# Hybrid decoder trunk on one core: score pieces of their own width, and a last tile whose second half runs in two pieces

## The chip, the cores and the metric

The kernel runs on one core of a Trainium2 chip. The core has five engines that each follow a stream of instructions of their own: PE (TensorE, matrix products; the loading of its weights is listed apart, as PEld), DVE (VectorE), ACT (ScalarE), POOL (GpSimd) and SP (SyncE, which here only issues DMAs). They meet through semaphores. The metric is the device time of one execution in microseconds (us), and the median of several executions is what counts.

## The reference

One layer of a decoder trunk over 1024 tokens of width 1024: differential softmax attention with 8 heads beside gated linear attention with 4 heads, both on one set of input projections, then one output projection, a normalisation, and the residual.

```python
h = rms_norm(x, pre_g)
z = h @ w_in                                  # all projections at once
# per attention head, for two maps (m = 0, 1), causal:
p_m = softmax(where(mask, q_m @ k_m.T, -inf))
oa  = (p_0 - lam * p_1) @ v                   # then rms_norm and a gate
ob  = gla_chunked(...)                        # then rms_norm and a gate
y = concatenate([oa, ob]) @ w_out             # 1024 x 2048 @ 2048 x 1024
return x + rms_norm(y, post_g)
```

## The kernel before

**Precision.** All large products are made from operands split into a high and a low part in the type fp32r, with three matmuls a product (high x high, low x high, high x low). Each matmul has 128 x 128 weights and streams up to 512 columns into one of the eight PSUM banks; a bank holds 128 x 512 fp32.

**Stages.** From 0 to 620 us the kernel normalises x and makes the input projections (by a Strassen-like scheme of seven products). From 620 to 925 us it runs attention. From 925 to 971 us it finishes the eight output tiles of 128 rows, and the rest is the end of the last of them.

**Attention** (620 to 925 us). Three generators are run against each other by `merge` (called at L1517 with their costs): `all_scores`, `all_values` and `out_early`. `scores(h, qb)` treats one block of 128 queries of one head: it needs `n = (qb + 1) * 128` keys, and `parts_of(n)` (L1114) says in which pieces of columns the scores are made. A piece is one PSUM bank `sc`. Each half of it takes two matmuls, `q` and `qs` against `k`. DVE then adds the mask and takes the minimum (L1168), ACT takes the exponential (L1178), DVE takes reciprocals (L1203), POOL scales the second map (L1204), and DVE subtracts it from the first (L1208). `parts_of` rounds a piece up to at least 256 columns: for `qb` 0 (n = 128) the matmuls are 256 columns wide, and for `qb` 4 (n = 640) the second piece is (512, 768). The readers of the bank take `e = min(b, n)`, so they never read the surplus columns. `values(h, j)` transposes the finished weights on PE (`wtr`, L114), and multiplies them with v into `po`; `out_early` makes the parts of the output projection that need no attention result (`ypart`).

The costs that `merge` weighs are `c = 0.08 + (e - a) / 512 * 0.56` per piece, worked out from `e`, not from the padded width. The instructions that `mm` issues stay in the order in which they are written; those of the other engines are placed by a scheduler, unless `pin` or `issue_after` ties them.

**End tiles.** `ENDS = [4, 5, 6, 7, 0, 1, 2, 3]` is the order in which tiles of rows are finished. `seed` copies what `out_early` had put aside for a tile into one of the eight PSUM banks in turn (`banks`), and `last_times` adds the last products: for one half `dh` (512 columns of the output, one bank) and one block `e` of the mixed heads, three matmuls of 512 columns. `finish(n)` (L1558) does this for e = 4 to 7 and both halves, 24 matmuls, called `yps` in the profile. After each half ACT squares the bank and sums the squares along the row (L1567, with a second small instruction that reads the sum). `rstd` (L1600) then makes the reciprocal root: Ln and Exp on ACT (L1602, L1603), and on DVE a half of the sum (L1604) and two steps of refinement (L1606, L1612). The minus one that the last refinement leaves is in `post_g`.

For the last two tiles the product with `post_g` does not wait for the root: DVE multiplies the bank by `post_g` into `y` (L1573 for the first half, L1577 for the second, tied behind the `half` of L1604), and then one operation per half scales y by the root and adds x (L1586). SP stores each half with a DMA of 256 KB (L1589).

Of the kernel before, what the change touches and what calls it, by code (L numbers as in the profile page):

```python
# [8 lines left out]
F32 = mybir.dt.float32  # L9
F32R = mybir.dt.float32r  # L10
AF = mybir.ActivationFunctionType
ALU = mybir.AluOpType
PSUM = bass.MemoryType.PSUM

P = 128
S = 1024
D = 1024
NT = S // P
# [4 lines left out]
EPS = 1e-6  # L23
# [8 lines left out]
def hymba_kernel(  # L32
# [20 lines left out]
    nc = tc.nc  # L53
    act, dve, pool, pe, sp = nc.scalar, nc.vector, nc.gpsimd, nc.tensor, nc.sync
# [4 lines left out]
    def cols(half):  # L59
        return slice(half * 512, half * 512 + 512)  # L60


    const = ctx.enter_context(tc.tile_pool(name="const", bufs=1))
# [46 lines left out]
    def mm(*a, **k):  # L110
        tc.keep_in_program_order(pe.matmul(*a, **k))  # L111
# [86 lines left out]
    y, z = len(pairs) - 2, len(pairs) - 1  # L198
# [910 lines left out]
    def pin(first, ins):  # L1109

        if first:
            tc.keep_in_program_order(ins)

    def parts_of(n):  # L1114
        return [(0, max(n, 256))] if n <= 512 else [(0, 512), (512, max(n, 768))]

    def load_v(h):
        v = [smp.tile([P, NT, P], F32R, tag="v", name=f"v{t}", bufs=4) for t in range(2)]
# [19 lines left out]
    w, used, scored, opened = {}, set(), [], {}  # L1138

    def scores(h, qb):  # L1140
# [5 lines left out]
        p1 = smp.tile([P, S], F32, tag="p1", name="p1", bufs=2)  # L1146
        for m, p in enumerate((p0, p1)):
            parts = parts_of(n)
            if h == DA_HEADS - 1 and (qb, m) in ((1, 1), (0, 0), (0, 1)):

# [237 lines left out]
    def out_early():  # L1388
# [63 lines left out]
        for st in ENDS[:2]:  # L1452
            for dh in range(2):
                for e in range(4, 7):
                    last_times(st, dh, parts_d[st], e)
                    yield 0.69
            if st == ENDS[0]:
                mix_pair(2)
                for dh in range(2):
                    yp = smp.tile([P, 512], F32, tag="yst", name="yp", bufs=2)  # L1460
                    sp.dma_start(yp, yd[ENDS[2]][dh])
                    yp2.append(yp)
                seed(ENDS[2], 0, SC[2], yp2[0])
# [10 lines left out]
    def early_ends():  # L1474

        for e in range(4, 7):
            last_times(ENDS[2], 0, parts_d[ENDS[2]], e)
        for n, st in enumerate(ENDS[:2]):
            last_part(ENDS[n + 1], parts_d[ENDS[n + 1]])
            if not n:  # L1480
                seed(ENDS[2], 1, PO, yp2[1])
            for dh in range(2):
                last_times(st, dh, parts_d[st], 7)


    parts_d, ps_d, yp2 = {}, {}, []
# [12 lines left out]
        opened[b] = None  # L1499
        pin(b not in Y, act.copy(ps, yp))  # L1500

    def last_times(st, dh, part, e):
        mh, ml = part
        hi, lo = wo[e]
        for i, (a, b) in enumerate(((mh, hi), (ml, hi), (mh, lo))):
            mm(
                ps_d[st, dh], a[:, e - 4, :], b[:, cols(dh)],
                start=False, stop=(e == 7 and i == 2), skip_group_check=True,
            )

    T = 8 * 36.0
    LAG = 21.0
    s_cost = sum(
        2 * sum(0.08 + (min(b, n) - a) / 512 * 0.56 for a, b in parts_of(n)) + 0.25 + n / 1024 * 1.4
        for n in range(P, S + 1, P)
    )
# [8 lines left out]
    fin = ctx.enter_context(tc.tile_pool(name="fin", bufs=3, reuse_waits="tile"))  # L1525
    post_g = fin.tile([P, D], F32, name="post_g", bufs=1)
# [4 lines left out]
    raws_d, yps, xts = {}, {}, {}  # L1531
# [26 lines left out]
    def finish(n):  # L1558
        st = ENDS[n]
        rows = slice(st * P, (st + 1) * P)  # L1560
        y = fin.tile([P, D], F32, name="y")
        ssq = const.tile([P, 4, 1], F32, tag="end_ssq", name="ssq", bufs=3)
        for dh in range(2):
            for e in range((8, 8, 7 - 3 * dh)[n] if n < 3 else 4, 8):
                last_times(st, dh, parts_d[st], e)
            junk = fin.tile([P, 512], F32, name="junk", bufs=2)
            pin(True, act.activation(  # L1567
                junk, ps_d[st, dh], AF.Square, scale=D**-0.5, accum_out=ssq[:, 2 + dh]
            ))
            if not dh:  # L1570
                dve.tensor_scalar(ssq[:, 0], ssq[:, 2], EPS, None, ALU.add)
                if n >= NT - LAST:
                    dve.tensor_tensor(y[:, cols(0)], ps_d[st, 0], post_g[:, cols(0)], ALU.mult)  # L1573
        ins = rstd(nc, ssq, ssq[:, 3], ssq[:, 0])[2]
        if n >= NT - LAST:
            with tc.issue_after(ins.ins):
                dve.tensor_tensor(y[:, cols(1)], ps_d[st, 1], post_g[:, cols(1)], ALU.mult)  # L1577
        for dh in range(2):
            cs = cols(dh)
            if n < NT - LAST:  # L1580
                dve.scalar_tensor_tensor(
                    y[:, cs], ps_d[st, dh], ssq[:, 1], post_g[:, cs], ALU.mult, ALU.mult
                )
                pool.dma_start(out[0, rows, cs], y[:, cs], accum_op=ALU.add)
            else:
                dve.scalar_tensor_tensor(  # L1586
                    y[:, cs], y[:, cs], ssq[:, 1], xts[n][:, cs], ALU.mult, ALU.add
                )
                sp.dma_start(out[0, rows, cs], y[:, cs])  # L1589

    for n in range(4):
        fetch(n)
    for n in range(NT):
        prime(n + 2)
        fetch(n + 4)
        finish(n)


def rstd(nc, t, s, eps, pin=None):

    pin = pin or (lambda ins: ins)
    pin(nc.scalar.activation(t[:, 1], s, AF.Ln, bias=eps))  # L1602
    exp = pin(nc.scalar.activation(t[:, 1], t[:, 1], AF.Exp, scale=-0.5))  # L1603
    half = pin(nc.vector.tensor_scalar(t[:, 2], s, eps, 0.5, ALU.add, ALU.mult))  # L1604
    if t.shape[2] == 1:
        pin(nc.vector.scalar_tensor_tensor(  # L1606
            t[:, 2], t[:, 1], t[:, 2], t[:, 1], ALU.mult, ALU.mult
        ))
    else:
        pin(nc.vector.tensor_tensor(t[:, 2], t[:, 2], t[:, 1], ALU.mult))  # L1610
        pin(nc.vector.tensor_tensor(t[:, 2], t[:, 2], t[:, 1], ALU.mult))
    last = nc.vector.scalar_tensor_tensor(  # L1612
        t[:, 1], t[:, 2], 1.5, t[:, 1], ALU.subtract, ALU.mult
    )
    return exp, pin(last), half
# [32 lines left out]
```

## Time and profile before

| | us |
|---|---|
| three executions | 978.89, 980.10, 977.54 |
| median | 978.89 |
| the profiled execution: its own time | 979.4 |
| the profiled execution: its span | 977.7 |

The span runs from the first to the last record, so 1.7 us of the profiled execution lie around it. The page's other views follow in the prediction, beside the sentences that use them. In a row of the timeline stand the start, the duration, the engine, the line, the operation, output <- inputs, and the tile's shape; a bracket at its end gives the idle time before it and who ended that. In a row of the page's groups stand the count, the busy time in us, the mean of one in ns, and the idle time before them. In a row of the windows stand the stretch and its length, then the busy time and count of PE, PEld, DVE, ACT and POOL, the granted clock of TensorE, the busy share of the DMA engines, and the GB/s that they moved.

### The profile page before, as it was taken

The page shows a single profiled execution, that of the slowest core. Times are in us where ns is not written, and L with a number is a line of the kernel's source. Part 1 is how long each engine was busy: PE and PEld are TensorE (multiplying, and loading weights), DVE is VectorE, ACT ScalarE, POOL GpSimd, SP SyncE. Part 2 cuts the span into 40 slices and gives each one's busy share as a digit, 9 for nine tenths or more (in the row PEclk, how much of TensorE's full clock was granted, in tenths as well). Part 3 has the DMA queues.
Part 4 walks back from the last instruction along what each step waited for, and adds up shares of the span by engine and source line. Part 5 has one row for each costly group of instructions (what it writes and reads, how often), then busy time and mean ns, then how long its engine had stood idle before and what let it go on. Part 6 is the DMA issues. An engine that isn't in the chain of part 4 may idle for free.

```text
span 977.7 us, 14802 instructions
## 1 busy us (share of the span) xinstructions
PE 956.5 (98%) x4866; PEld 807.0 (83%) x4866; DVE 738.5 (76%) x1450; ACT 590.2 (60%) x1152; POOL 210.2 (21%) x289
## 2 busy tenths in 40 slices
PE   6999999999999999999989999999999999999997
PEld 4888888878888888888878888888888888888875
DVE  5996576889989776778787766677787778887755
ACT  7741232347466467756577774367667667787764
POOL 5420100011211121112110000022232233443232
PEclk9999999999999999999999999999999999999999
DMA  8255543758865775899986569998575678994658
GB/s 305 83 161 160 194 143 99 223 167 268 278 234 191 265 249 195 268 279 301 310 258 194 172 216 320 396 329 253 165 245 181 199 265 245 327 267 99 198 156 156
DMA packets 144556, 220.37 MB, mean 225 GB/s; under 512 B 14704, under 2 KB 78704, under 8 KB 144384
## 3 DMA queue, kind: packets, MB, share of 16 engines
q1 hardware_dynamic: 130144, 175.38, 56.3%
q0 software_dynamic: 14336, 44.05, 15.2%
q8 instruction: 38, 0.62, 0.3%
q14 instruction: 38, 0.31, 0.1%
HBM read 133.93 MB, written 88.60 MB: 228 GB/s over the span
## 4 chain that ended last, share of the span: by engine, by line
PE 91%; ACT 3%; DVE 3%; DMA 2%; issue 1%; DVEq 0%; POOL 0%; ACTq 0%; SPq 0%
PE x L111 16%; PE v L111 16%; PE ypart L111 12%; PE z L111 11%; PE y L111 11%; PE sc L111 7%; PE po L111 5%; PE yps L111 4%; PE wtr L114 3%; PE gpo L111 2%; PE kv L111 1%; PE gkl_ps L111 1%; PE ms L111 1%; DMA m_raw<-mixd 1%; PE pa L111 1%
## 5 line engine op out<-in xcount | busy, mean ns | idle before, releaser
L1178 ACT ACTIVATE p<-p,stt 128x896 f32<-128x896 f32 (+7 forms) x128 | 99.3, 777 | 47.1 <-DVE stt L1168 44.2
L335 DVE TENSOR_TENSOR w<-w_raw,w 128x512 fp32r<-128x512 f32 x134 | 91.8, 688 | 31.5 <-ACT w L333 31.0
L333 ACT CAST w<-w_raw 128x512 fp32r<-128x512 f32 x134 | 82.5, 619 | 42.7 <-PE y L111 19.4
L1204 POOL TENSOR_SCALAR p<-p,stt,lam 128x1024 f32<-128x1024 f32 (+3 forms) x64 | 54.9, 858 | 207.9 <-DVE stt L1203 202.1
L1168 DVE CUSTOM_DVE_ANT_0 p<-sc,maskt 128x512 f32<-128x512 f32 (+3 forms) x128 | 74.4, 584 | 31.6 <-PE sc L111 30.9
L111 PE MATMUL y<-h_hi,w 128*128 128x512 f32 x320 | 80.6, 394 | 0.0
L111 PE MATMUL x<-s_hi,w 128*128 128x512 f32 x320 | 80.5, 394 | 0.0
L111 PE MATMUL z<-s_hi,w 128*128 128x512 f32 x320 | 80.4, 393 | 0.0
L111 PE MATMUL ypart<-wo_hi,m_hi 128*128 128x512 f32 x192 | 79.4, 413 | 0.6 <-ACT yst L1385 0.5
L111 PE MATMUL v<-w,s_hi 128*128 128x512 f32 x256 | 79.0, 390 | 0.1
L111 PE MATMUL ypart<-wo_hi,m_lo 128*128 128x512 f32 x192 | 75.5, 393 | 0.0
L111 PE MATMUL ypart<-wo_lo,m_hi 128*128 128x512 f32 x192 | 75.5, 393 | 0.0
L488 ACT COPY s<-x 128x512 f32<-128x512 f32 x60 | 35.0, 583 | 63.1 <-PE x L111 62.9
L111 PE MATMUL sc<-k,q 128*128 128x512 f32 (+1 forms) x192 | 71.0, 372 | 0.4 <-DVE stt L1168 0.4
L111 PEld LDWEIGHTS z<-s_hi,w 128*128 128x128 f32 x320 | 59.1, 188 | 11.7
L111 PEld LDWEIGHTS x<-s_hi,w 128*128 128x128 f32 x320 | 59.1, 188 | 11.7
L111 PEld LDWEIGHTS y<-h_hi,w 128*128 128x128 f32 x320 | 59.0, 188 | 11.6
L111 PE MATMUL sc<-k,qs 128*128 128x512 f32 (+1 forms) x192 | 66.6, 349 | 0.0
L285 ACT CAST w<-w_block 128x1024 fp32r<-128x1024 f32 x24 | 25.0, 1051 | 66.0 <-PE v L111 43.1
L257 DVE TENSOR_TENSOR w_raw<-w_raw 128x512 f32<-128x512 f32 x80 | 55.2, 690 | 9.9 <-DMA w_raw<-in_w_in_dram 8.9
L111 PE MATMUL v<-w,h_hi 128*128 128x512 f32 x192 | 60.3, 401 | 0.4 <-ACT h_hi L582 0.4
L1208 DVE SCALAR_TENSOR_TENSOR p<-p,stt,p 128x1024 f32<-128x1024 f32 (+3 forms) x64 | 52.5, 824 | 6.7 <-POOL p L1204 6.5
(233 smaller groups left out, 2379.5 us busy)
## 6 DMA issues: line engine op xcount, KB each, us to landing
w_raw<-in_w_in_dram SPq DMA_DIRECT2D x40, 512.0 KB, 5.2
w_block<-in_w_in_dram SPq DMA_DIRECT2D x16, 512.0 KB, 4.4
wo_raw<-in_w_out_dram POOLq DMA_DIRECT2D x32, 256.0 KB, 4.2
wo_d<-wo_hi POOLq DMA_DIRECT2D x32, 256.0 KB, 4.4
wo_d<-wo_raw POOLq DMA_DIRECT2D x32, 256.0 KB, 4.8
qs<-q_d SPq DMA_DIRECT2D x32, 256.0 KB, 8.1
k<-k_d SPq DMA_DIRECT2D x16, 512.0 KB, 9.1
q<-q_d SPq DMA_DIRECT2D x16, 512.0 KB, 6.8
```

Of the source, the lines that this page charges most:

```text
L111: tc.keep_in_program_order(pe.matmul(*a, **k))
L114: tc.keep_in_program_order(pe.transpose(dst, src, ident))
L257: dve.tensor_tensor(dst, a, b, ALU.subtract)
L285: act.copy(w[0], src)
L333: act.copy(w[0], src)
L335: split_last[:] = [dve.tensor_tensor(w[1], src, fp(w[0]), ALU.subtract)]
L488: act.copy(b[k], ps)
L1168: ins = dve.tensor_tensor_reduce(p[:, a:e], sc[:, : e - a], maskt[:, NZ + P - (e - a) :] if last else maskt[:, : e - a], 1.0, 3e38 if i == ...
L1178: act.activation(p[:, :n], p[:, :n], AF.Exp, bias=st[:, m : m + 1], scale=-1.0, accum_out=st[:, 2 + m : 3 + m],)
L1204: pool.tensor_scalar(p1[:, :n], p1[:, :n], st[:, 5:6], lam, ALU.mult, ALU.mult)
L1208: dve.scalar_tensor_tensor(p0[:, :n], p0[:, :n], st[:, 4:5], p1[:, :n], ALU.mult, ALU.subtract)
```

## The change

It has two parts.

**Part 1.** `parts_of` returns the pieces without padding. A piece of 128 columns is then made with matmuls of 128 columns. Head 7 keeps its written exceptions of 512 columns for `(qb, m)` = (1, 1), (0, 0) and (0, 1).

**Part 2.** The last tile (n = 7) no longer goes through `finish` but through `finish_last`. Its second half is made in two pieces of 256 columns, each with twelve matmuls of 256 columns. Each piece has its own square and its own product with `post_g`. After the root is there, the final scaling is divided: ACT scales columns 0 to 191 into a tile `z`, POOL adds x to it, and DVE treats columns 192 to 639 and 640 to 1023 as before. SP stores 640 columns (320 KB) and then 384 (192 KB).

```diff
     def parts_of(n):
-        return [(0, max(n, 256))] if n <= 512 else [(0, 512), (512, max(n, 768))]
+        return [(0, n)] if n <= 512 else [(0, 512), (512, n)]
...
-    def last_times(st, dh, part, e):
+    def last_times(st, dh, part, e, a=0, b=512):
         mh, ml = part
         hi, lo = wo[e]
-        for i, (a, b) in enumerate(((mh, hi), (ml, hi), (mh, lo))):
+        at = slice(512 * dh + a, 512 * dh + b)
+        for i, (m, w) in enumerate(((mh, hi), (ml, hi), (mh, lo))):
             mm(
-                ps_d[st, dh], a[:, e - 4, :], b[:, cols(dh)],
+                ps_d[st, dh][:, a:b], m[:, e - 4, :], w[:, at],
                 start=False, stop=(e == 7 and i == 2), skip_group_check=True,
             )
...
         ssq = const.tile([P, 4, 1], F32, tag="end_ssq", name="ssq", bufs=3)
+        if n == NT - 1:
+            return finish_last(st, rows, y, ssq, xts[n])
...
+    def finish_last(st, rows, y, ssq, xt):
+        junk = [fin.tile([P, 512], F32, name="junk", bufs=2) for _ in range(2)]
+        part = const.tile([P, 3], F32, name="last_ssq")
+        r, ys = ssq[:, 1], [(0, 0, 512), (1, 0, 256), (1, 256, 512)]
+        for i, (dh, a, b) in enumerate(ys):
+            for e in range(4, 8):
+                last_times(st, dh, parts_d[st], e, a, b)
+            ps = ps_d[st, dh][:, a:b]
+            pin(True, act.activation(
+                junk[dh][:, a:b], ps, AF.Square, scale=D**-0.5, accum_out=part[:, i : i + 1]
+            ))
+            if i == 1:
+                dve.scalar_tensor_tensor(
+                    ssq[:, 0], part[:, 0:1], EPS, part[:, 1:2], ALU.add, ALU.add
+                )
+            if i < 2:
+                at = slice(512 * dh + a, 512 * dh + b)
+                last = dve.tensor_tensor(y[:, at], ps, post_g[:, at], ALU.mult)
+        ins = rstd(nc, ssq, part[:, 2:3], ssq[:, 0])[2]
+        with tc.issue_after(ins.ins):
+            dve.tensor_tensor(y[:, 768:], ps, post_g[:, 768:], ALU.mult)
+        z = fin.tile([P, 192], F32, name="z", bufs=1)
+        act.activation(z, y[:, :192], AF.Copy, scale=r)
+        pool.tensor_tensor(y[:, :192], z, xt[:, :192], ALU.add)
+        for a, b in ((192, 640), (640, 1024)):
+            dve.scalar_tensor_tensor(y[:, a:b], y[:, a:b], r, xt[:, a:b], ALU.mult, ALU.add)
+        sp.dma_start(out[0, rows, :640], y[:, :640])
+        sp.dma_start(out[0, rows, 640:], y[:, 640:])
```

In the changed program the Square stands on L1602, the sum of parts on L1606, the products with `post_g` on L1611 (the first two pieces) and L1614 (the third), the new ACT and POOL steps on L1616 and L1617, the last scaling on L1619 and the stores on L1620 and L1621; `rstd` is at L1634 (Ln), L1635 (Exp), L1636, L1638 and L1644.

What the two parts move is seen in the order of the built programs. First PE in the attention stage, a piece of the difference between the two programs. `sc` is the bank of a scores piece, `k_5898` and `q_5894` are buffers of one head's keys and queries, and `wtr` is a transposition for `values`.

```order
 L111 MATMUL sc<-k_5896,q_5894 128x512
 L111 MATMUL sc<-k_5896,qs_5900 128x512
-L111 MATMUL sc<-k_5898,q_5894 128x256
-L111 MATMUL sc<-k_5898,qs_5900 128x256
+L111 MATMUL sc<-k_5898,q_5894 128x128
+L111 MATMUL sc<-k_5898,qs_5900 128x128
 L114 MATMUL wtr<-ident,p_6292 128x128
 L114 MATMUL wtr<-ident,p_6197 128x128
```

Nothing moved: the pair of `qb` 4 stands where it stood, and each of its matmuls is 128 columns narrower. The same holds of all 60 matmuls that the padding had widened (28 of `qb` 0 in heads 0 to 6, and 32 of `qb` 4 in heads 0 to 7). Behind them five neighbouring pairs of rows on DVE and two on ACT have changed places.

Second PE at the end of the program, around the start of the last tile's second half. The bracket names the counters that an instruction waits for; DVE_49 counts what DVE has finished. Before:

```order
L111 MATMUL yps<-wo_hi,m_lo 128x512 [waits DVE_49]
L111 MATMUL yps<-wo_lo,m_hi 128x512
L111 MATMUL yps<-wo_hi,m_hi 128x512 [waits Activation_49]
L111 MATMUL yps<-wo_hi,m_lo 128x512
L111 MATMUL yps<-wo_lo,m_hi 128x512
```

Of the change, around the start of the third piece, twelve matmuls after the row that waits for Activation_49:

```order
L111 MATMUL yps<-wo_hi,m_hi 128x256
L111 MATMUL yps<-wo_hi,m_lo 128x256
L111 MATMUL yps<-wo_lo,m_hi 128x256
L111 MATMUL yps<-wo_hi,m_hi 128x256 [waits DVE_49]
L111 MATMUL yps<-wo_hi,m_lo 128x256
L111 MATMUL yps<-wo_lo,m_hi 128x256
```

The row with the wait is the third piece's first matmul. It is new: the value of the counter that it waits for is reached when the second piece's product with `post_g` (L1611) is finished, since both pieces lie in one PSUM bank.

Third DVE, from the end of the last tile's first half to the end of the program. Before:

```order
L1571 TENSOR_SCALAR ssq<-ssq 128x1 [waits Activation_49]
L1573 TENSOR_TENSOR y<-yps,post_g 128x512 [waits DMASW7_49,DMASW6_49]
L1604 TENSOR_SCALAR ssq<-ssq 128x1 [waits DVE_49,Activation_49]
L1577 TENSOR_TENSOR y<-yps,post_g 128x512
L1606 SCALAR_TENSOR_TENSOR ssq<-ssq 128x1 [waits DVE_49,Activation_49]
L1612 SCALAR_TENSOR_TENSOR ssq<-ssq 128x1 [waits DVE_49]
L1586 SCALAR_TENSOR_TENSOR y<-y,ssq,xt 128x512 [waits DMAHW4_49,DVE_49]
L1586 SCALAR_TENSOR_TENSOR y<-y,ssq,xt 128x512
```

Of the change:

```order
L1611 TENSOR_TENSOR y<-yps,post_g 128x512 [waits DMASW7_49,DMASW6_49,Activation_49]
L1606 SCALAR_TENSOR_TENSOR ssq<-last_ssq 128x1 [waits Activation_49]
L1611 TENSOR_TENSOR y<-yps,post_g 128x256
L1636 TENSOR_SCALAR ssq<-last_ssq,ssq 128x1 [waits Activation_49]
L1614 TENSOR_TENSOR y<-yps,post_g 128x256
L1638 SCALAR_TENSOR_TENSOR ssq<-ssq 128x1 [waits DVE_49,Activation_49]
L1644 SCALAR_TENSOR_TENSOR ssq<-ssq 128x1 [waits DVE_49]
L1619 SCALAR_TENSOR_TENSOR y<-y,ssq,xt 128x448 [waits DMAHW4_49,DVE_49]
L1619 SCALAR_TENSOR_TENSOR y<-y,ssq,xt 128x384
```

The second piece's product with `post_g` stands behind the sum of parts, which waits for ACT's square of that piece; the product that stood behind the last half now covers 256 columns; and the two scalings cover 832 columns of the 1024. The other 192 go through ACT and POOL. SP's first store of the last tile waits for both DVE and POOL, its second for DVE alone.

## The prediction

> **What bounds the kernel now.** The first view is the busy time of the engines, the second the chain that ended last.
>
> ```profile
> PE 956.5 (98%) x4866; PEld 807.0 (83%) x4866; DVE 738.5 (76%) x1450; ACT 590.2 (60%) x1152; POOL 210.2 (21%) x289
> PE 91%; ACT 3%; DVE 3%; DMA 2%; issue 1%; DVEq 0%; POOL 0%; ACTq 0%; SPq 0%
> ```
>
> PE is busy for 98% of the span and holds 91% of the chain: an edit counts by what it takes from or adds to PE's stream, and by what it does after PE's last matmul. The two parts lie in two stages, so the third view is the windows of these two.
>
> ```profile
> 620.00:925.00 305.00, 303.34 (x1748) 262.60 (x1747) 230.47 (x632) 210.39 (x468) 100.37 (x118) 1.00 0.77 241
> 971.20:977.70 6.50, 0.00 (x0) 0.00 (x0) 2.51 (x6) 1.19 (x4) 0.00 (x0) 0.77 0.21 81
> ```
>
> In attention PE idles for 305.00 - 303.34 = 1.66 us in all, at a granted clock of 1.00: fewer PE cycles there shorten the kernel directly. In the last 6.5 us PE does nothing, and a chain through ACT, DVE and SP sets the end; the timeline shows it.
>
> ```profile
> 968.31 0.39 PE L111 MATMUL yps<-wo_hi,m_hi 128*128 128x512 f32 x1
> ...
> 970.81 0.39 PE L111 MATMUL yps<-wo_lo,m_hi 128*128 128x512 f32 x1
> 971.23 0.60 ACT L1567 ACTIVATE junk<-yps 128x512 f32<-128x512 f32 x1 [2.03 <-PE yps L111]
> 971.73 0.19 ACT L1567 ACTIVATION_READ_ACCUMULATOR junk<-yps 128x1 f32 x1
> 971.95 0.30 ACT L1602 ACTIVATE ssq<-ssq 128x1 f32<-128x1 f32 x1
> 971.95 0.21 DVE L1604 TENSOR_SCALAR ssq<-ssq 128x1 f32<-128x1 f32 x1 [1.95 <-ACT junk L1567]
> 972.08 0.68 DVE L1577 TENSOR_TENSOR y<-yps,post_g 128x512 f32<-128x512 f32 x1
> 972.28 0.20 ACT L1603 ACTIVATE ssq<-ssq 128x1 f32<-128x1 f32 x1
> 972.68 0.21 DVE L1606 SCALAR_TENSOR_TENSOR ssq<-ssq 128x1 f32<-128x1 f32 x1
> 972.93 0.16 DVE L1612 SCALAR_TENSOR_TENSOR ssq<-ssq 128x1 f32<-128x1 f32 x1
> 973.12 1.41 DVE L1586 SCALAR_TENSOR_TENSOR y<-y,ssq,xt 128x512 f32<-128x512 f32 x2
> 973.90 0.99 SPq L1589 DMA_DIRECT2D out_dram<-y  x2
> ```
>
> The first two rows are the first and the last of the second half's twelve matmuls. The square takes 971.23 to 971.92, the root 971.95 to 973.09, the two scalings 0.705 us each, and the stores are issued at 973.90 and at the second scaling's end, 973.12 + 1.41 = 974.53.
>
> **Part 1: narrower scores.** 60 matmuls go from 256 to 128 columns. What does one save?
>
> ```profile
> 748.02 0.28 PE L111 MATMUL sc<-k,q 128*128 128x256 f32 x1
> 748.14 0.28 PE L111 MATMUL sc<-k,qs 128*128 128x256 f32 x1
> 748.26 0.40 PE L111 MATMUL ypart<-wo_hi,m_hi 128*128 128x512 f32 x1
> 651.78 0.22 PE L111 MATMUL po<-wt_lo,v 128*128 128x128 f32 x1
> 651.84 0.45 PE L111 MATMUL ypart<-wo_hi,m_hi 128*128 128x512 f32 x1
> 652.12 0.40 PE L111 MATMUL ypart<-wo_hi,m_lo 128*128 128x512 f32 x1
> L111 PE MATMUL po<-wt_hi,v 128*128 128x128 f32 x64 | 10.7, 249 | 0.0
> ```
>
> Starts are what counts, since matmuls overlap. A matmul of 256 columns takes a slot of (748.26 - 748.02) / 2 = 0.12. The one of 128 columns at 651.78 lets the next start after 0.06, but that one, of 512 columns, then holds the stream for 0.28 where such a matmul otherwise takes (970.81 - 968.31) / 11 = 0.227. The two together took 652.12 - 651.78 = 0.34, so the narrow one cost 0.34 - 0.227 = 0.113: each matmul brings 128 columns of weights, and their load shows from behind. The saving is 0.12 - 0.113 = 0.007 each, 60 x 0.007 = **0.4 us**. Its bounds are 0 (weights cover everything) and 60 x 0.06 = 3.6 (the start alone); I take the pair's value, because in both programs the scores' neighbours are matmuls with weights of their own.
>
> [...]
>
> DVE and ACT read the same columns as before, and the merge weighs the same costs. The few neighbours that change places on DVE and ACT I cost at nothing: PE's 1.66 us of idle time in 305 us says that its stream is full behind them. Without that cover one swap would cost at most one DVE operation, near 0.7.
>
> **Part 2: the last tile.** It adds twelve matmuls (24 of 256 columns for 12 of 512: 24 x 0.12 = 2.88 against 12 x 0.227 = 2.72) and a wait of PE. Rows for its prices:
>
> ```profile
> 943.68 0.50 PE L111 MATMUL yps<-wo_hi,m_hi 128*128 128x512 f32 x1 [0.21 <-ACT yps L1500]
> 944.01 0.40 PE L111 MATMUL yps<-wo_hi,m_lo 128*128 128x512 f32 x1
> 961.40 0.20 ACT L1603 ACTIVATE ssq<-ssq 128x1 f32<-128x1 f32 x1
> 961.64 0.22 DVE L1606 SCALAR_TENSOR_TENSOR ssq<-ssq 128x1 f32<-128x1 f32 x1 [0.35 <-ACT ssq L1603]
> L1246 DVE TENSOR_TENSOR wt_lo<-wtr,wt_hi 128x384 fp32r<-128x384 f32 x32 | 17.7, 552 | 1.7 <-ACT wt_hi L1245 1.3
> L1273 ACT COPY o<-po 128x256 f32<-128x256 f32 x32 | 11.6, 364 | 7.7 <-PE po L111 7.7
> L1368 ACT CAST m_hi<-gate 128x128 fp32r<-128x128 f32 x8 | 2.3, 293 | 0.1
> ```
>
> The second piece starts where the second half did, 968.31; its twelfth matmul starts 11 x 0.12 later, 969.63, and ends 0.28 after that, 969.91. ACT squares it from 969.94. The sum is read 0.26 later than the start (0.50 at 512 columns, less 0.24: the slope of ACT is (0.60 - 0.364) / 256 columns), and is there at 970.20 + 0.19 = 970.39. DVE adds the parts at 970.42 and multiplies by `post_g` from 970.55, 0.13 later as at 971.95 and 972.08; 256 columns take 0.42 (0.552 at 384, 0.68 at 512), to 970.97. (The first half's product waits for ACT too, but so did L1571 ahead of it.) The third piece lies in the same bank, and its first matmul waits for that: it starts at 971.00, not at 969.75. **PE stands for 1.25 us**, with all twelve matmuls of the third piece queued behind the waiting one and the whole end behind these. The first matmul after a wait holds the stream 0.10 longer (944.01 - 943.68 = 0.33 for 0.227). So the last matmul starts at 971.00 + 0.10 + 11 x 0.12 = 972.42 and ends at 972.70, where it ended at 970.81 + 0.39 = 971.20: **1.50 later**.
>
> From there the chain is shorter. Square 972.73, sum there at 973.18, Ln 973.21, Exp 973.54. In before, L1606 came 0.40 after Exp's start (972.28 to 972.68), because DVE was still at the product of 512 columns; at the other tile it came 0.24 after (961.40 to 961.64). The product now has 256 columns and ends by 973.76, so L1638 starts at 973.78, L1644 at 974.03, and the root can be used at 974.22: 1.10 after the 973.12 of before.
>
> Then the scaling. ACT's 192 columns cost 0.35 (0.293 at 128, with the slope above), to 974.57. DVE's 832 columns take 832 / 1024 x 1.41 = 1.15, to 975.40 or so. POOL's addition of 192 columns is not in the trace; its nearest rows:
>
> ```profile
> L606 POOL TENSOR_TENSOR f1hi<-h_hi,h_lo 128x512 f32<-128x512 f32 x4 | 5.0, 1290 | 3.0 <-DVE h_lo L583 3.0
> L640 POOL TENSOR_TENSOR f1hi<-s,f1hi 128x512 f32<-128x512 f32 x4 | 6.7, 1672 | 11.9 <-DVE s L630 11.9
> L1204 POOL TENSOR_SCALAR p<-p,stt,lam 128x128 f32<-128x128 f32 x8 | 4.4, 553 | 7.0 <-DVE stt L1203 7.0
> ```
>
> In proportion to columns it is 192 / 512 x 1.29 = 0.48, the low end; an operation of 128 columns with one tensor input already takes 0.553. The high end is a whole row of 512 columns, 1.29 or 1.67, if the addition is held up. I take 0.75, between the 0.553 and the low row plus a start-up of some 0.3. POOL ends at 974.60 + 0.75 = 975.35, and SP issues the larger store at 975.40, **1.50 after** the 973.90 of before; the smaller one, 0.36 behind it (974.89, the stores' end, less 974.53), at 975.75, which is 1.2 after the 974.53 of before.
>
> Which of the two sets the end?
>
> ```profile
> 974.00:974.50 0.50, 0.00 (x0) 0.00 (x0) 0.50 (x1) 0.00 (x0) 0.00 (x0) 1.00 0.00 0
> 974.50:975.00 0.50, 0.00 (x0) 0.00 (x0) 0.03 (x1) 0.00 (x0) 0.00 (x0) 0.70 0.53 209
> 975.00:975.50 0.50, 0.00 (x0) 0.00 (x0) 0.00 (x0) 0.00 (x0) 0.00 (x0) 0.50 0.97 373
> 975.50:976.00 0.50, 0.00 (x0) 0.00 (x0) 0.00 (x0) 0.00 (x0) 0.00 (x0) 0.50 1.07 418
> 976.00:976.50 0.50, 0.00 (x0) 0.00 (x0) 0.00 (x0) 0.00 (x0) 0.00 (x0) 0.50 0.14 49
> ```
>
> 0.5 x (209 + 373 + 418 + 49) = 524 KB, both stores, ran without a break from some 0.8 after the first issue, with the DMA engines fully busy in the middle: the end follows the first issue, and the same bytes are moved after the change. So I take 1.5 and keep 1.2 as the other end. The first row has the clock still at 1.00, three us after the last matmul, so a wait of 1.25 us need not slow the third piece.
>
> **Sum.** On the profiled execution's own 979.4 (span 977.7 and 1.7 around it): -0.4 + 1.5 = +1.1, 980.5. That execution lay 0.5 above the median of 978.89 shown, so over the median the forecast is **980.0**. A measurement can tell about 0.3%, 2.9 us, from no change.
>
> **The rivals.**
> *The bank costs no wait.* If the third piece ran on at once, all behind it would come 1.35 earlier than in the sum (the wait and the 0.10 after it), so the larger store at 975.40 - 1.35 = 974.05: 0.15 after 973.90, and 978.89 - 0.4 + 0.15 = 978.6. For it: PE so far starts its second half while DVE reads the first, without idling; that is another bank. Against: the waiting row in PE's order. Chance 0.10.
> *POOL is held up.* DVE's scalings with two inputs run beside the addition; at 1.29 to 1.67 it ends 0.5 to 0.9 later, and the larger store with it: 980.5 to 980.9. For it: L640 and L606, of one shape, differ by 0.38. Against: those two are full rows of 512 columns, and POOL's `p` row of 128 columns at 0.553 ran in a stage where DVE is busy for three quarters of the time. Chance 0.25. [...]
> *Narrow matmuls run at the speed of their columns.* Then part 1 saves 60 x 0.06 = 3.6: 978.89 - 3.6 + 1.5 = 976.8. For it: the start 0.06 after 651.78. Against: the 0.28 that follows. Chance 0.06.
> *Slower: fp32r below 256 columns goes in two passes.* The place is part 1's matmuls, the price one more pass each.
>
> ```profile
> L111 PE MATMUL gpo<-gan,gv 128*128 128x128 f32 x128 | 23.4, 274 | 0.0
> ```
>
> These are plain fp32 products; the program issues 64, and 128 are recorded. If the narrow scores did so too, 60 x 0.113 = 6.8 (a slot each) would be added in place of the 0.4 taken off: 978.89 + 6.8 + 1.5 = 987.2. It decides for slower from (2.9 - 1.5) / 0.113, some 13 doubled matmuls, on. Against it: `po<-wt_hi,v` at 128x128, fp32r, stands in 64 records for its 8 heads x 4 x 2 calls, one each. Chance 0.04.
>
> **How the numbers follow.** The forecast has 0.53, the rivals 0.10, 0.25, 0.06 and 0.04, and 0.02 is left for anything else. The three runs of before lie up to 1.3 from their median; 1.1 of that below the first rival's 978.6 and above the second's 980.9 gives 977.5 to 982.0, which leaves out the last two rivals. Within 0.3% (976.0 to 981.8) are the forecast, the first two rivals and most of the third, less the outer part of their spread: 0.90. Faster by more than that needs a part of the third: 0.03. Slower has the fourth and the upper edge of the second: 0.07.
>
> **What would show it.** In the changed profile: starts of narrow scores followed by a late next matmul (a pair's cost near 0.11); `yps` of 256 columns in two groups of twelve, with an idle time of 1.1 to 1.4 us before the second, put down to DVE; the root about 0.24 after Exp; POOL's addition at 0.5 to 1.7; the larger store issued after POOL's end. The prediction is wrong if there is no idle time before the third piece, if the stage from 620 to 925 shrinks by over 1 us, or if narrow scores have two records each.

## The result, and the profile after

| | kernel before | changed kernel |
|---|---|---|
| median | 978.21 us (977.11 to 980.1, 4 runs) | 991.42 us (990.28 to 991.95, 4 runs) |
| the profiled execution: its own time | 979.4 us | 991.76 us |
| the profiled execution: its span | 977.7 us | 990.1 us |
| ratio | | 1.0134, 95% interval 1.0108 to 1.0159 |

The change costs 13 us; the forecast was 980.0 with a range up to 982.0. First the page of the changed kernel, engines and chain:

```profile
PE 970.6 (98%) x4878; PEld 807.7 (82%) x4878; DVE 740.2 (75%) x1451; ACT 590.9 (60%) x1155; POOL 210.6 (21%) x290
PE 93%; DMA 2%; DVE 2%; ACT 2%; issue 1%; POOL 0%; DVEq 0%; SPq 0%; ACTq 0%
```

PE has only twelve more matmuls (4878 for 4866) and 14.1 us more busy time, and its share of the chain grew. So the loss is in PE's own stream. Where? The view of the tile `sc` gives the first and the last start of the scores, and so cuts the execution in three. Before:

```profile
L111 PE MATMUL sc<-k,q x192: 274/389/499, 623.7 to 917.7; 128*128 128x512 f32 x99, 128*128 128x256 f32 x61, 128*128 128x384 f32 x32
```

And of the changed kernel:

```profile
L111 PE MATMUL sc<-k,q x192: 219/389/499, 634.9 to 927.5; 128*128 128x512 f32 x99, 128*128 128x384 f32 x32, 128*128 128x256 f32 x31, 128*128 128x128 f32 x30
```

| stretch | before | after | difference |
|---|---|---|---|
| up to the first score | 623.7 | 634.9 | +11.2 |
| first to last score | 294.0 | 292.6 | -1.4 |
| last score to last matmul (970.81, 982.67) | 53.1 | 55.2 | +2.1 |
| last matmul to the end (977.7, 990.1) | 6.9 | 7.4 | +0.5 |

(The scores' stretch differs by up to 1.1 us among the traces below that have the same scores, so little hangs on its -1.4.) Eleven of the twelve us are lost before attention, in a stage whose instructions the change does not touch: PE's order there is the same in both programs. The chain of waits shows how, for pieces of that stage in which PE runs twelve matmuls of 512 columns on end (start, length, what). Before:

```profile
604.43 2.72 PE y L111 x12
607.15 2.72 PE x L111 x12
609.87 2.72 PE y L111 x12
```

After:

```profile
612.32 2.80 PE x L111 x12
615.12 2.80 PE y L111 x12
617.92 2.80 PE x L111 x12
```

Every matmul takes 2.80 / 12 = 233 ns in place of 2.72 / 12 = 227, at a granted clock of 1.00 in both. From one start to the next, over the 2341 steps of this kind that the changed kernel's trace has before attention, the mean is 233.2 ns, and 227.2 before; 6 ns x 2341 = 14 us. 11.2 of it are seen at the first score; the rest went into waits that PE had in that stage before: between its first matmul and the first score it idled for 4.7 us before, and for 1.9 after.

And the tail that the prediction was about, in the timeline of the changed kernel:

```profile
979.89 0.28 PE L111 MATMUL yps<-wo_lo,m_hi 128*128 128x256 f32 x1
980.21 0.38 ACT L1602 ACTIVATE junk<-yps 128x256 f32<-128x256 f32 x1 [0.74 <-PE yps L111]
980.72 0.16 DVE L1606 SCALAR_TENSOR_TENSOR ssq<-last_ssq 128x1 f32<-128x1 f32 x1 [0.52 <-ACT junk L1602]
980.79 0.42 DVE L1611 TENSOR_TENSOR y<-yps,post_g 128x256 f32<-128x256 f32 x1
981.26 0.39 PE L111 MATMUL yps<-wo_hi,m_hi 128*128 128x256 f32 x1 [1.09 <-DVE y L1611]
981.49 0.28 PE L111 MATMUL yps<-wo_hi,m_lo 128*128 128x256 f32 x1
...
982.67 0.28 PE L111 MATMUL yps<-wo_lo,m_hi 128*128 128x256 f32 x1
982.98 0.38 ACT L1602 ACTIVATE junk<-yps 128x256 f32<-128x256 f32 x1 [2.30 <-PE yps L111]
983.82 0.20 ACT L1635 ACTIVATE ssq<-ssq 128x1 f32<-128x1 f32 x1
984.05 0.22 DVE L1638 SCALAR_TENSOR_TENSOR ssq<-ssq 128x1 f32<-128x1 f32 x1
984.50 0.46 ACT L1616 ACTIVATE z<-y,ssq 128x192 f32<-128x192 f32 x1 [0.48 <-DVE ssq L1644]
984.50 1.59 DVE L1619 SCALAR_TENSOR_TENSOR y<-y,ssq,xt 128x448 f32<-128x448 f32 x2
985.09 0.59 POOL L1617 TENSOR_TENSOR y<-z,xt 128x192 f32<-128x192 f32 x1 [10.18 <-ACT z L1616]
985.71 0.33 SPq L1620 DMA_DIRECT2D out_dram<-y  x1
986.13 0.38 SPq L1621 DMA_DIRECT2D out_dram<-y  x1
```

PE stands for 981.26 - 979.89 - 0.12 = 1.25 us for DVE's product in the same bank, as forecast; the row itself counts 1.09, since the busy time of the twelfth matmul reaches into it. Up to the issue of the stores the rest of the tail is near the forecast too. What was not in it is the 233.

**A lead.** Of what the change adds, one line acts on the whole program: `part = const.tile([P, 3], ..., name="last_ssq")`. Its 12 bytes a partition take 32 in the pool of constants, and that pool lies below all other tiles that are placed from the lower side of SBUF, the core's memory for all tiles but the PSUM banks. In the built program one of the five buffers of the weights `w` of the projections lay at 60,416 bytes in each partition before (a multiple of 512) and lies at 60,448 now; the other four moved by 32 too. The tiles placed from the upper side (`h_hi`, `s_hi` and their low parts, the `wo` that the attention and end stages read) did not move. In a projection one operand of each matmul comes from the lower side and one from the upper.

### The profile page after: what moved, and what is told of

It reads as the page before. It is cut to its first block, busy times and chain, and to the rows that moved or that the text cites. A ratio compares the mean times of both kernels' runs of the same rounds, so it can differ in the third digit from the quotient of the medians.

```text
span 990.1 us, 14829 instructions
## 1 busy us (share of the span) xinstructions
PE 970.6 (98%) x4878; PEld 807.7 (82%) x4878; DVE 740.2 (75%) x1451; ACT 590.9 (60%) x1155; POOL 210.6 (21%) x290
## 4 chain that ended last, share of the span: by engine, by line
PE 93%; DMA 2%; DVE 2%; ACT 2%; issue 1%; POOL 0%; DVEq 0%; SPq 0%; ACTq 0%
PE x L111 17%; PE v L111 16%; PE ypart L111 12%; PE z L111 11%; PE y L111 11%; PE sc L111 6%; PE po L111 5%; PE yps L111 4%; PE wtr L114 3%; PE gpo L111 3%; PE kv L111 1%; DMA mixd<-o 1%; DMA m_raw<-mixd 1%; PE gkl_ps L111 1%; PE pa L111 1%; PE ms L111 1%
## 5 line engine op out<-in xcount | busy, mean ns | idle before, releaser
L257 DVE TENSOR_TENSOR w_raw<-w_raw 128x512 f32<-128x512 f32 x80 | 55.2, 690 | 10.8 <-DMA w_raw<-in_w_in_dram 9.8
L111 PEld LDWEIGHTS v<-w,s_hi 128*128 128x128 f32 x256 | 47.9, 188 | 12.1 <-DVE v_st L433 0.5
```

Source lines behind the costliest of these rows:

```text
L257: dve.tensor_tensor(dst, a, b, ALU.subtract)
```

## The experiments

**First four: the address, and the parts by themselves.** gap32 and gap64 are the kernel before with an unused tile; nothing else differs in any engine's stream.

```diff
-    raws_d, yps, xts = {}, {}, {}
+    raws_d, yps, xts = {}, {}, {}; const.tile([P, 8], F32, name="gap")     # gap32; [P, 16] in gap64
```

> The kernel before with one unused tile of 32 bytes a partition in the pool of constants; every engine's instructions and their order are the same, but all tiles that are placed behind that pool lie 32 bytes further, so that 3984 of 4658 matmuls read weights, or moving columns, or both from an address 32 past a multiple of 64 (384 before, all of them transposes). Theory A (the changed kernel lost its time because its new constant tile moved the operands off multiples of 64): the steps of the 512-column matmuls before attention go from 227 to 233 ns, some 1920 x 6.6 ns = 12 us more, 989 to 991. Theory B (the loss comes from the narrow score matmuls): no change, 978. Theory C (it comes from the longer program or the last tile): no change, 978.

Measured: 990.5 (989.9 to 990.83), 1.0135 of before (1.0118 to 1.0152). An unused tile of 32 bytes costs as much as the whole change. As the causes of this loss theories B and C fall.

> The same with an unused tile of 64 bytes: all addresses move, but by a whole 64. Theory A: 978, steps of 227 ns. A rival form of A, that any move of the tiles costs the time (a conflict between some two addresses rather than their place within 64 bytes): 985 or more. B and C: 978.

Measured: 989.93 (988.93 to 990.54), 1.013 (1.0115 to 1.0145). The plain form of theory A falls as well: a multiple of 64 is as bad. The chain of gap64 in the projections:

```profile
614.38 2.80 PE y L111 x12
617.18 2.80 PE x L111 x12
```

Part 1 alone:

```diff
-        return [(0, max(n, 256))] if n <= 512 else [(0, 512), (512, max(n, 768))]
+        return [(0, n)] if n <= 512 else [(0, 512), (512, n)]
```

> Part 1 of the change alone (score pieces without padding), addresses as before. Theory A: between 974.5 and 978, the prediction's term of -0.4 with its bounds 0 and -3.6. Theory B: 985 or more, with two records for a narrow matmul.

Measured: 976.94 (975.25 to 980.85), 1.0002 (0.9987 to 1.0016). Narrower scores move the time by nothing that can be seen, and theory B falls a second time. Its view of `sc`:

```profile
L111 PE MATMUL sc<-k,q x192: 218/389/499, 622.0 to 915.4; 128*128 128x512 f32 x99, 128*128 128x384 f32 x32, 128*128 128x256 f32 x31, 128*128 128x128 f32 x30
```

30 narrow records of `q` for 30 instructions: these fp32r matmuls of 128 columns leave one record each, and no second pass is seen. In the trace, a narrow pair of `q` and `qs` followed by `ypart` ends 10 to 17 ns earlier than the wide one (medians of 8 pairs with the same neighbours in both kernels), and one followed by transpositions 37 ns earlier (15 pairs): some 5 to 19 ns a matmul, 0.7 us over these 23 of the 30 pairs. Not all of it reaches the time: from the first score to the last it takes 293.5 us in the mean of the seven traces with wide pieces (293.1 to 294.0), and 293.4 in that of the six with narrow ones (292.6 to 293.7). Part of it goes into one wait of PE late in the stage, of a transposition (`wtr`) for ACT's L1296. It is 0.3 us at most with wide pieces (0.28 before), and 0.6 to 1.0 in five of the six traces with narrow ones (0.79 in narrow_only; the changed kernel has next to none): PE comes earlier and waits longer.

The whole change with a tile of 64 bytes:

```diff
-        part = const.tile([P, 3], F32, name="last_ssq")
+        part = const.tile([P, 16], F32, name="last_ssq")
```

> The whole change, with the new constant tile last_ssq made 64 bytes wide instead of 12 (which take 32), so that the tiles behind it lie at multiples of 64 again. Theory A: 978.2 - 0.4 + 1.5 = 979.3, within 977 to 981, the forecast for the change. Theories B and C: 991, as the changed kernel.

Measured: 991.43 (991.24 to 992.46), 1.0148 (1.0133 to 1.0163): as gap64, no repair. What was open after these four: does a larger granule matter, or the distance between the two operands?

**Next four: granule or distance.** gap128 and gap256 are larger unused tiles. moved64 moves both sides up by 64 bytes, so that every operand lies off a multiple of 128, and the distance between them is that of before:

```diff
-    pool.memset(edge.tile([P, 120], F32, name="edge"), 0.0)
+    pool.memset(edge.tile([P, 104], F32, name="edge"), 0.0)                # with the gap of 64
```

> The kernel before with an unused tile of 128 bytes a partition in the pool of constants, all instructions the same. gap64 was as slow as gap32, so a multiple of 64 is not enough. Theory A1 (an operand that starts off a multiple of some larger granule costs each matmul; before, both operands of nearly all of them lie at multiples of 512): 990 if the granule is 256 or 512, 977 if it is 128. Theory A2 (weights and moving columns cost time where their addresses differ by something other than a multiple of 512, whatever each is by itself): 990.

Measured: 990.06 (989.86 to 992.18), 1.0137 (1.011 to 1.0165).

> The same with 256 bytes. A1: 990 with a granule of 512, 977 with 256 or 128. A2: 990 with a difference of 512 that matters, 977 with 256.

Measured: 976.4 (974.09 to 979.29), 0.9989 (0.9973 to 1.0006). The loss is gone at 256. Its chain in the projections:

```profile
607.00 2.72 PE y L111 x12
609.72 2.72 PE x L111 x12
```

> The kernel before with both sides of SBUF moved up by 64 bytes: the unused tile of 64 bytes for the side that grows from below, and the tile at the upper end (edge) 64 bytes smaller. Every matmul of 512 columns then has both operands 64 past a multiple of 128, and the distance between its operands is what it was. A1: 990, as gap64. A2: 977.

Measured: 977.66 (975.98 to 980.28), 1.0006 (0.9988 to 1.0024). Its chain:

```profile
605.29 2.72 PE x L111 x12
608.01 2.72 PE y L111 x12
```

This decides for the distance, A2. Both operands of the projections' matmuls are 64 bytes past a multiple of 128 here, and the steps are 227 ns; in gap64 one of the two is, and they are 233. 32, 64 and 128 bytes of relative move cost the time, 256 do not.

The whole change, with the new tile taken from the last pool, which shifts no operand:

```diff
-        part = const.tile([P, 3], F32, name="last_ssq")
+        part = fin.tile([P, 3], F32, name="last_ssq", bufs=1)
```

> The whole change, with last_ssq taken from the last pool (fin) in place of the pool of constants: the order on every engine is that of the changed kernel, all tiles behind the constants lie where they lay before. A1 and A2: 977.3 - 0.4 + 1.5 = 978.4, within 976 to 980 (part 2's wait of PE is in the changed profile at 1.25 us), with steps of 227 ns. If the added instructions make the loss in some way that gap32 and gap64 only resemble: 991.

Measured: 978.78 (977.62 to 981.67), 1.0019 (1.0003 to 1.0035). One tile declared in another pool brings back some 11 of the 13 us. What is left, near 1.9 us, is the change proper.

**Last three: one operand alone, and the tail.** gap_in_fin puts the unused tile of 64 bytes in front of the last pool.

```diff
-    fin = ctx.enter_context(tc.tile_pool(name="fin", bufs=3, reuse_waits="tile"))
+    fin = ctx.enter_context(tc.tile_pool(name="fin", bufs=3, reuse_waits="tile")); fin.tile([P, 16], F32, name="gap", bufs=1)
```

> The kernel before with an unused tile of 64 bytes at the start of the last pool (fin), all instructions the same. Of the matmuls of 512 columns only 96, the last ones of the program, get weights (m_hi, m_lo) that lie 64 bytes further, against columns (wo) that stay. Theory A2 (the distance between a matmul's weights and its columns, off a multiple of 256 bytes, costs that matmul about 6.6 ns): steps of 227 ns in the projections as before, and 233 in the last 96, 0.6 us in all. A3 (the loss comes from something else between the two sides of SBUF, as from the other engines' writes beside PE's reads): 227 in the last 96 too.

Measured: 978.12, one run, beside 978.11 for the kernel before: 0.6 us can't be seen in the time. The steps can. Its chain in the projections, and then its timeline in the last tile:

```profile
606.10 2.72 PE x L111 x12
608.82 2.72 PE y L111 x12
```

```profile
966.93 0.40 PE L111 MATMUL yps<-wo_hi,m_hi 128*128 128x512 f32 x1
...
969.26 0.40 PE L111 MATMUL yps<-wo_hi,m_lo 128*128 128x512 f32 x1
969.50 0.39 PE L111 MATMUL yps<-wo_lo,m_hi 128*128 128x512 f32 x1
```

(969.50 - 966.93) / 11 = 234 ns in the last tile, where before had 227, and 227 in the projections: the loss follows the matmuls whose weights moved against their columns, and only them. A3 falls.

own_bank gives the third piece a PSUM bank of its own:

```diff
+        if n == NT - 1:
+            seed(st, 2, banks[0], yps[n][1])
...
-                ps_d[st, dh][:, a:b], m[:, e - 4, :], w[:, at],
+                ps_d[st, dh if k is None else k][:, a:b], m[:, e - 4, :], w[:, at],
...
-                last_times(st, dh, parts_d[st], e, a, b)
-            ps = ps_d[st, dh][:, a:b]
+                last_times(st, dh, parts_d[st], e, a, b, i)
+            ps = ps_d[st, i][:, a:b]
```

> The whole change with last_ssq in fin, and the third piece in a PSUM bank of its own (seeded by one more ACT copy, whose upper half is used). Prediction's step that PE stands 1.25 us for the second piece's product in the same bank: that idle time goes, and from the first matmul of the last tile's second half to the end of the program it takes 11.49 - 1.34 = 10.15 us (11.49 in both_in_fin, 9.39 in the kernel before); 978.78 - 1.3 = 977.4. If the idle time has another cause, it stays, and so does 11.49.

Measured: 977.83 (975.62 to 978.7), 0.9998 (0.9983 to 1.0013). The last matmul starts at 966.52, 23 steps of 0.12 after the first of the half at 963.77, without idle time between the pieces, and the program ends at 973.92: 10.15 us after that first one, the forecast to the digit. The wait was the shared bank. (The medians alone can't show it: the interval of both_in_fin overlaps this one.)

own_bank_no_pool leaves the scaling of the last tile to DVE, as in the kernel before:

```diff
-        z = fin.tile([P, 192], F32, name="z", bufs=1)
-        act.activation(z, y[:, :192], AF.Copy, scale=r)
-        pool.tensor_tensor(y[:, :192], z, xt[:, :192], ALU.add)
-        for a, b in ((192, 640), (640, 1024)):
+        for a, b in ((0, 512), (512, 1024)):
             dve.scalar_tensor_tensor(y[:, a:b], y[:, a:b], r, xt[:, a:b], ALU.mult, ALU.add)
-        sp.dma_start(out[0, rows, :640], y[:, :640])
-        sp.dma_start(out[0, rows, 640:], y[:, 640:])
+            sp.dma_start(out[0, rows, a:b], y[:, a:b])
```

> own_bank, with DVE scaling all 1024 columns in two halves and two stores of 256 KB as in the kernel before, so that POOL does nothing in the last tile. In both_in_fin POOL's closing drain ends 3.6 us after its addition, and the program's closing meeting of the engines starts 0.54 after SP was ready for it. Theory D (a late POOL operation sets the end through this drain): from the first matmul of the second half to the end 9.2 us, 0.2 less than in the kernel before, and 976.9. If the stores' shape (320 and 192 KB) sets the end, the same gain; the trace tells the two apart by when POOL enters the meeting: D says within 0.05 of SP. If neither: 10.15 - 0.3 = 9.9.

Measured: 975.92 (974.43 to 978.65), 0.9978 (0.9964 to 0.9992), and 976.95 - 967.77 = 9.18 us from the first matmul of the half to the end. The records at the end of the four traces, in us. DRAIN is an instruction that each engine has at the end of its stream. "SP ready" is the start of SP's DRAIN behind its waits for the stores' landing; "POOL opens" is POOL's first step in the closing meeting of the engines, behind its own DRAIN:

```
                   POOL's addition   POOL's DRAIN         SP ready   POOL opens   end
before             -                 963.76 to 971.31     976.93     976.96       977.70
both_in_fin        974.38, 0.59      974.35 to 978.57     978.07     978.61       979.35
own_bank           968.95, 0.59      968.92 to 973.14     972.63     973.18       973.92
own_bank_no_pool   -                 964.08 to 971.51     976.18     976.22       976.95
```

With POOL's addition the program ends behind POOL's DRAIN, 0.54 after SP was ready; without it POOL follows SP by 0.04. Theory D holds for that half us. Of the 10.15 - 9.18 = 0.97 us between own_bank and own_bank_no_pool it is 0.51; the other 0.45 or so is SP's, which is ready 8.41 us after the first matmul of the half, in place of 8.86. The later store is issued 0.19 earlier (6.03 for 6.22) and SP sees it landed 2.08 after its issue in place of 2.34; whether the stores' shape has a part in that was not told apart.

This kernel has the lowest ratio of all that ran, and its interval lies below 1, 0.8 to 3.5 us ahead of the kernel before. (It overlaps that of gap256, which changes no instruction.) By the trace its gain is small: 0.21 us in the tail, and of part 1's 0.7 what reaches the time. So at most the low end of the interval is explained.

## Why the prediction was wrong

**The step that failed** is the sum: "-0.4 + 1.5 = +1.1". It priced each instruction that the change adds or narrows, and took all other work of PE as unchanged. The list in "Part 2: the last tile" leaves the new tile out altogether. None of the rivals had it either; rival four named a loss of the right sign, 987.2, by a mechanism that isn't there (narrow_only has one record a matmul). The runs put in its place: the 32 bytes of `last_ssq` move the lower operands against the upper ones, each matmul of 512 columns in the projections takes 6 ns more, and that is 11.2 us by the first score. gap32, which adds those 32 bytes and nothing else, costs 990.5 - 977.33 = 13.2 us, as much as the whole change.

The rest, by its own steps:

- **Part 1, -0.4 us, bounds 0 and -3.6.** Right beside `ypart`: one record each, 5 to 8 ns saved. Beside transpositions it is 18, which the one pair that was read could not show; some 0.7 in all by the steps. That the load of the weights is what fills the narrow slot was the author's reading of that pair (the load at 651.78 lasts 0.19, the next matmul starts at 651.84); no run isolates it. "Fewer PE cycles there shorten the kernel directly" holds only in part: in narrow_only some 0.5 us of them come back in PE's wait for L1296, and the time can tell nothing (0.9987 to 1.0016).
- **PE stands for 1.25 us.** Right: 1.25 in the changed kernel; own_bank shows its cause by taking it away.
- **The chain behind it.** The last matmul came 4.10 us after the first of the half in both_in_fin (967.86, 971.96; forecast 972.42 - 968.31 = 4.11), L1638 0.24 after Exp's start, the larger store 7.13 after (forecast 7.09).
- **POOL's 0.75.** It took 0.59. The second rival had the right pair of engines, but the one that is seen to lose is DVE. The rows of both_in_fin, and behind them its view of L1619 (count, shortest, median and longest in ns, first and last start):

```profile
973.79 0.45 ACT L1616 ACTIVATE z<-y,ssq 128x192 f32<-128x192 f32 x1 [0.48 <-DVE ssq L1644]
973.79 1.59 DVE L1619 SCALAR_TENSOR_TENSOR y<-y,ssq,xt 128x448 f32<-128x448 f32 x2
974.38 0.59 POOL L1617 TENSOR_TENSOR y<-z,xt 128x192 f32<-128x192 f32 x1 [9.94 <-ACT z L1616]
974.99 0.33 SPq L1620 DMA_DIRECT2D out_dram<-y  x1
975.42 0.38 SPq L1621 DMA_DIRECT2D out_dram<-y  x1
L1619 DVE SCALAR_TENSOR_TENSOR y<-y,ssq,xt x2: 685/838/991, 973.8 to 974.4; 128x448 f32<-128x448 f32 x1, 128x384 f32<-128x384 f32 x1
```

  DVE's 832 columns take 1.59 where the prediction had 1.15, and where 1024 columns take 1.42 in own_bank_no_pool:

```profile
972.36 1.42 DVE L1618 SCALAR_TENSOR_TENSOR y<-y,ssq,xt 128x512 f32<-128x512 f32 x2
973.14 1.00 SPq L1619 DMA_DIRECT2D out_dram<-y  x2
```

  The first scaling, of 448 columns, runs beside ACT's step and takes 0.69. The second, of 384, starts at 974.39, with POOL's addition, and takes 0.99, more than the 0.75 of 512 columns in own_bank_no_pool. So the sharing of the scaling gains nothing: it takes 192 columns from DVE, and the 384 beside POOL take 0.24 longer than 512 without it (in the changed kernel too: 0.69 and 0.99, the second from 985.10, POOL's addition from 985.09). That the addition is what makes DVE late is read from this overlap alone. Whether POOL's addition is late too these rows don't show, since no run has it alone. The larger store waited for POOL (974.97), the smaller one for DVE (975.38).
- **+1.5 for the tail.** A term was missing in size: from the first matmul of the half to the end it is 11.49 - 9.39 = 2.10. 1.54 of it stands at the larger store's issue, as worked out, and 1.59 where SP is ready (978.07 - 967.86 = 10.21 for 976.93 - 968.31 = 8.62). The other half us is POOL's DRAIN, which the prediction did not look at since no row of the page counts it.
- **The total without the shift.** both_in_fin gives +1.9 (0.3 to 3.4, from the interval on 977.1), against +1.1. Its own terms are +2.1 in the tail, less what of part 1's 0.7 reaches the time.

## What to carry to other kernels

A tile is an instruction to the allocator too. Before pricing a change by its instructions, compare where the operands of the hot matmuls lie in the two built programs; a few bytes in a pool that lies below others can outweigh all that the edit does (32 bytes cost 13.2 us here, the edit without the shift 1.9). Put small late tiles into the last pool, or round the first pool's growth to what the hot operands need (256 bytes here). And work given to an idle engine near the end is paid once more when that engine must finish before the program may (0.51 us here, for POOL's DRAIN).

## What the runs showed of the hardware

- **The distance between weights and columns counted in the time.** With the weights' and the columns' addresses in a partition as far apart as before, or 256 bytes further, a run of 512-column matmuls in the projections steps at 227 ns; with 32, 64 or 128 bytes more between them at 232 to 233. Where both are moved together, by 64, it stays at 227. What makes the distance cost time is not shown. Attention does not test this: there both operands of the scores lie on the lower side and both of `ypart` on the upper, so the unused tiles leave their distance as it was. The steps of 512 columns in attention have a mean near 234 ns in the kernel before and with the shift (233.4 before, 234.6 in the changed kernel), at distances that are multiples of 256, and why they are longer than 227 there is open. Whether it is the distance to a matmul's own weights that counts, or to the next one's, whose load of 0.19 us starts while it runs, was not told apart, since all weights of a stage move together.
- **The small POOL operation had a long end.** 587 ns of addition go with a DRAIN that ends 4.2 us after the addition's start, in three traces alike (the DRAIN lasts 4.22 in both_in_fin, in own_bank and in the changed kernel). POOL's next DRAIN, behind no work of its own, takes 0.1 us in both_in_fin. Without the addition the DRAIN stands behind POOL's last DMA issues and is even longer (7.5 us before, 7.4 in own_bank_no_pool), but it ends over 4 us before SP is ready, so it costs nothing there. What the DRAIN waits for is not shown.
